# Instance norm on one core: equal 4 MB units in six slots, against 4 MB and 6 MB units in four

## The chip, the cores and the metric

The kernel runs on one core of a Trainium2 chip. The metric is the device time of one execution in microseconds (us). Three runs of the kernel before took 626.85, 626.98 and 627.24 us; the median is 626.98.

The core has five engines that work side by side and meet at semaphores: TensorE (PE, matrix products), VectorE (DVE), ScalarE (ACT), GpSimd (POOL) and SyncE (SP, which here only issues transfers). Data moves between the large memory (HBM) and the on-chip memory (128 partitions) by 16 DMA engines. SP, ACT and POOL each issue transfers into a queue of their own.

## What is computed

```python
# x: [4, 8, 16, 256, 256] float32, gamma: [8, 16] float32
mu = x.mean(axis=(3, 4), keepdims=True)
var = ((x - mu) ** 2).mean(axis=(3, 4), keepdims=True)
out = (x - mu) / np.sqrt(var + 1e-5) * gamma[None, :, :, None, None]
```

There are 512 channels (4 x 8 x 16) of 65,536 numbers, 256 KB each. Every channel gets its own mean and variance, and one of 128 values of gamma. 134 MB are read and 134 MB written, and a channel must be read whole before its first number can be written.

## The kernel before

A **unit** is 16 consecutive channels, 4 MB, held as a tile of 128 partitions by 8192 numbers: a channel is 8 partitions, and a partition holds one row of 32 KB that is contiguous in HBM. There are 32 units and six slots for them (`slots`, L45); unit `u` uses slot `u % 6`.

The program issues the first six loads at once (L56 and L57): units 1 and 3 on ACT's queue, the rest on SP's. A write of 8 KB to the output (`touch`, L54) and the load of gamma (L55) go through POOL's queue. POOL then makes `navg` (L63 to L73), a 128 by 128 matrix that holds -1/65536 where two partitions belong to the same channel, and 0 elsewhere. DVE repeats gamma (L80) and PE spreads it to a column per unit position (L85), copied to `g_col` (L91).

The loop over units is written out in one order for each engine (the schedule is manual; every engine does its own instructions in program order):

1. DVE sums each row (L106) while ACT squares each row and sums that (L107, the squares themselves go to `junk`).
2. PE multiplies `navg` by the two columns of sums (L115): every partition gets minus its channel's mean and minus its mean square.
3. DVE makes minus the variance (L116), ACT its square root (L120), DVE the reciprocal (L124) and the product with gamma (L126).
4. DVE adds minus the mean and multiplies by the scale, in place (L135). In unit 0 alone ACT does the last 3/8 of it (L132), beside DVE.
5. ACT issues the store of the unit (L139), and SP the load of unit `u + 6` (L48). That load waits until the store has landed, since it overwrites the slot.

Of the kernel before, what the change touches and what calls it, by code (L numbers as in the profile page):

```python
# [1 line left out]

# [4 lines left out]

F32 = mybir.dt.float32
U8 = mybir.dt.uint8
ALU = mybir.AluOpType  # L10
ACTF = mybir.ActivationFunctionType
AX = mybir.AxisListType


@with_exitstack
def kernel(
    ctx: ExitStack,
    tc: tile.TileContext,
    x: bass.AP,
    gamma: bass.AP,  # L20
    out: bass.AP,
):
    nc = tc.nc
    B, G, C, H, W = x.shape
    P = nc.NUM_PARTITIONS
    HW = H * W
    n_ch = B * G * C
    S = 8
    K = P // S
    F = HW // S  # L30
    U = n_ch // K
    NG = (G * C) // K
    AHEAD = 6
    assert HW % S == 0 and (G * C) % K == 0

    xv = x.rearrange("b g c h w -> (b g c h w)").rearrange("(u p f) -> u p f", p=P, f=F)
    ov = out.rearrange("b g c h w -> (b g c h w)").rearrange("(u p f) -> u p f", p=P, f=F)
    gv = gamma.rearrange("g c -> (g c)")

    data = ctx.enter_context(tc.tile_pool(name="data", bufs=1))  # L40
    singles = ctx.enter_context(tc.tile_pool(name="singles", bufs=1))
    psum = ctx.enter_context(tc.tile_pool(name="psum", bufs=4, space=bass.MemoryType.PSUM))
    ctx.enter_context(tc.manual_schedule())

    slots = [data.tile([P, F], F32, name=f"xt{i}") for i in range(AHEAD)]  # L45

    def load(u, queue):
        queue.dma_start(out=slots[u % AHEAD][:], in_=xv[u])  # L48


    g_row = singles.tile([1, G * C], F32, name="g_row")
    touch = singles.tile([16, 128], F32, name="touch")
    nc.vector.memset(touch[:], 0.0)  # L53
    nc.gpsimd.dma_start(out=ov[0][0::S, 0:128], in_=touch[:])  # L54
    nc.gpsimd.dma_start(out=g_row[:], in_=gv[None, :])  # L55
    for u in range(AHEAD):  # L56
        load(u, nc.scalar if u in (1, 3) else nc.sync)  # L57

    eps_t = singles.tile([P, 1], F32, name="eps_t")
    nc.gpsimd.memset(eps_t[:], 1e-5)  # L60
    one = singles.tile([1, 1], F32, name="one")
    nc.gpsimd.memset(one[:], 1.0)
    navg = singles.tile([P, K, S], F32, name="navg")  # L63
    nc.gpsimd.memset(navg[:], -1.0 / HW)  # L64
    nc.gpsimd.affine_select(  # L65
        out=navg[:], in_=navg[:], pattern=[[-S, K], [0, S]], compare_op=ALU.is_ge,
        fill=0.0, base=0, channel_multiplier=1,
    )
    nc.gpsimd.affine_select(  # L69
        out=navg[:], in_=navg[:], pattern=[[S, K], [0, S]], compare_op=ALU.is_ge,  # L70
        fill=0.0, base=S - 1, channel_multiplier=-1,
    )
    navg_w = navg[:].rearrange("p k s -> p (k s)")  # L73
    root_eps = singles.tile([P, 1], F32, name="root_eps")
    nc.scalar.activation(out=root_eps[:], in_=eps_t[:], func=ACTF.Sqrt)  # L75
    g_rep = singles.tile([1, NG, K, S], F32, name="g_rep")
    g_ps = psum.tile([P, NG], F32, name="g_ps", bufs=1)
    g_col = singles.tile([P, NG], F32, name="g_col")

    nc.vector.tensor_copy(  # L80
        out=g_rep[:],
        in_=g_row[:].rearrange("o (n k) -> o n k", n=NG).unsqueeze(3).to_broadcast([1, NG, K, S]),
    )
    for n in range(NG):
        nc.tensor.matmul(  # L85
            out=g_ps[:, n : n + 1],
            lhsT=g_rep[:, n].rearrange("o k s -> o (k s)"),
            rhs=one[:],
            start=True, stop=True,
        )  # L90
    nc.vector.tensor_copy(out=g_col[:], in_=g_ps[:])  # L91

    junk = singles.tile([P, F], U8, name="junk")

    st = singles.tile([P, U, 2], F32, name="st")
    nvar = singles.tile([P, U], F32, name="nvar")
    std = singles.tile([P, U], F32, name="std")
    rstd = singles.tile([P, U], F32, name="rstd")
    scale = singles.tile([P, U], F32, name="scale")

    shift = singles.tile([P, 1], F32, name="shift")

    squares = []
    for u in range(U):
        t = slots[u % AHEAD]
        nc.vector.reduce_sum(out=st[:, u, 0:1], in_=t[:], axis=AX.X)  # L106
        square = nc.scalar.activation(  # L107
            out=junk[:], in_=t[:], func=ACTF.Square, accum_out=st[:, u, 1:2],
        )
        if u:  # L110

            tc.declare_no_dep(square.ins, squares[-1].ins, reason="junk, ordered by the root between")
        squares.append(square)
        ps = psum.tile([P, 2], F32, name="ps")
        nc.tensor.matmul(out=ps[:], lhsT=navg_w, rhs=st[:, u], start=True, stop=True)  # L115
        nc.vector.tensor_scalar(  # L116
            out=nvar[:, u : u + 1], in0=ps[:, 0:1], scalar1=ps[:, 0:1],
            scalar2=ps[:, 1:2], op0=ALU.mult, op1=ALU.add,
        )
        nc.scalar.activation(  # L120
            out=std[:, u : u + 1], in_=nvar[:, u : u + 1], func=ACTF.Sqrt,
            bias=eps_t[:], scale=-1.0,
        )
        nc.vector.reciprocal(out=rstd[:, u : u + 1], in_=std[:, u : u + 1])  # L124
        g = u % NG
        nc.vector.tensor_mul(  # L126
            out=scale[:, u : u + 1], in0=rstd[:, u : u + 1], in1=g_col[:, g : g + 1],
        )
        cut = F * 5 // 8 if u == 0 else F
        if cut < F:  # L130
            nc.vector.tensor_mul(out=shift[:], in0=ps[:, 0:1], in1=scale[:, u : u + 1])  # L131
            nc.scalar.activation(  # L132
                out=t[:, cut:], in_=t[:, cut:], func=ACTF.Identity, bias=shift[:], scale=scale[:, u : u + 1],
            )
        nc.vector.tensor_scalar(  # L135
            out=t[:, :cut], in0=t[:, :cut], scalar1=ps[:, 0:1], scalar2=scale[:, u : u + 1],
            op0=ALU.add, op1=ALU.mult,
        )
        nc.scalar.dma_start(out=ov[u], in_=t[:])  # L139
        if u + AHEAD < U:  # L140
            load(u + AHEAD, nc.sync)


# [1 line left out]
_INS = ['x', 'gamma']  # L145
_OUTS = [((4, 8, 16, 256, 256), 'float32')]


# [23 lines left out]
```

## Time and profile before

| | value |
|---|---|
| median of the runs | 626.98 us |
| the profiled execution: span, first to last instruction | 625.2 us |
| DVE busy | 441.8 us (71%) |
| ACT busy | 241.8 us (39%) |
| PE busy | 21.4 us (3%) |
| POOL busy | 2.4 us |
| bytes moved by the DMA engines | 268.46 MB, mean 429 GB/s |
| packets on ACT's queue (q10) and on SP's (q1) | 4896 and 4320 |
| 4 MB store, issue to landing, median | 62.5 us |
| 4 MB load on SP, issue to landing, median | 38.5 us |

The page cuts the span into 40 equal slices of 15.6 us and gives, for each, the busy share of every engine in tenths and what the DMA engines moved. A **packet** is what one DMA engine moves at a time; here it is a row of a tile. After the rows of a transfer, each of the 16 engines sends a small completion packet of 4 bytes. A group of instructions has its busy time, the mean time of one, and the idle time of its engine before them with what ended it. The times of the profiled execution are those of its span; the runs' times also hold what lies around the span.

### The profile page before, as it was taken

The numbers are of one execution on the slowest core, as the hardware profiler recorded it, in microseconds if no ns is written. First come the engines' busy times: TensorE is split into PE (matmuls) and PEld (weight loads), VectorE is DVE, ScalarE is ACT, GpSimd is POOL, SyncE is SP. The second block draws the span as 40 slices with busy tenths as digits, with TensorE's granted clock in tenths as the row PEclk, the third lists the DMA queues.
The fourth block names the chain that finished last, engine by engine and source line by source line (L and its number), as shares of the span: only waits on it lengthen the run. The fifth ranks groups of instructions, "written<-read, shape, count | busy, mean of one in ns | idle before, by whom it ended". The sixth has DMA issues, their size and how long they took to land.

```text
span 625.2 us, 635 instructions
## 1 busy us (share of the span) xinstructions
PE 21.4 (3%) x80; PEld 19.5 (3%) x80; DVE 441.8 (71%) x164; ACT 241.8 (39%) x99; POOL 2.4 (0%) x11
## 2 busy tenths in 40 slices
PE   0200000000000000000000000000000000000000
PEld 0200000000000000000000000000000000000000
DVE  0589999998776687666786767867668676687730
ACT  0464444444443244432344423444224442244400
POOL 1000000000000000000000000000000000000000
DMA  8999999999999999999999999999999999999998
GB/s 370 436 407 432 436 436 436 436 436 430 423 436 434 434 428 434 434 436 436 436 436 428 426 436 436 432 430 434 434 436 436 436 436 421 432 436 434 434 430 367
DMA packets 9282, 268.46 MB, mean 429 GB/s; under 512 B 1072, under 2 KB 1088, under 8 KB 1088
## 3 DMA queue, kind: packets, MB, share of 16 engines
q10 hardware_dynamic: 4896, 142.61, 52.9%
q1 hardware_dynamic: 4320, 125.83, 46.8%
q0 software_dynamic: 64, 0.01, 0.0%
q14 instruction: 2, 0.02, 0.0%
HBM read 134.22 MB, written 134.23 MB: 429 GB/s over the span
## 4 chain that ended last, share of the span: by engine, by line
another core or an unknown queue 61%; DMA 17%; DVE 15%; SPq 1%; PE 1%; issue 0%; ACT 0%
DMA xt<-in_x_dram 10%; DVE st L106 10%; DMA out_dram<-xt 8%; DVE xt L135 5%; SPq L48 1%; PE ps L115 1%; ACT std L120 0%; DVE nvar L116 0%; DVE rstd L124 0%; DVE scale L126 0%; DVE shift L131 0%
## 5 line engine op out<-in xcount | busy, mean ns | idle before, releaser
L106 DVE TENSOR_REDUCE st<-xt 128x1 f32<-128x8192 f32 x32 | 277.9, 8684 | 102.2 <-DMA xt<-in_x_dram 102.2
L107 ACT ACTIVATE junk<-xt 128x8192 uint8<-128x8192 f32 x32 | 225.0, 7030 | 272.0 <-DMA xt<-in_x_dram 233.8
L135 DVE TENSOR_SCALAR xt<-xt,ps,scale 128x8192 f32<-128x8192 f32 (+1 forms) x32 | 144.0, 4500 | 1.1
L120 ACT ACTIVATE std<-nvar,eps_t 128x1 f32<-128x1 f32 x32 | 9.4, 295 | 79.4 <-DVE nvar L116 79.4
L115 PE MATMUL ps<-st,navg 128*128 128x2 f32 x64 | 17.8, 348 | 557.3 <-DVE st L106 557.3
L115 PEld LDWEIGHTS ps<-st,navg 128*128 128x128 f32 x64 | 16.0, 310 | 559.1 <-issue 546.2
L116 DVE TENSOR_SCALAR nvar<-ps 128x1 f32<-128x1 f32 x32 | 9.2, 286 | 23.8 <-PE ps L115 23.8
L124 DVE RECIPROCAL rstd<-std 128x1 f32<-128x1 f32 x32 | 5.2, 163 | 11.6 <-ACT std L120 11.6
L80 DVE COPY g_rep<-g_row 1x1024 f32<-1x1024 f32 x1 | 0.7, 681 | 14.4 <-DMA g_row<-in_gamma_dram 14.4
L107 ACT ACTIVATION_READ_ACCUMULATOR junk<-xt 128x1 f32 x32 | 6.0, 186 | 0.0
L126 DVE TENSOR_TENSOR scale<-rstd,g_col 128x1 f32<-128x1 f32 x32 | 5.1, 158 | 1.1
L85 PE MATMUL g_ps<-one,g_rep 1*128 1x1 f32 x16 | 3.5, 347 | 16.3 <-DVE g_rep L80 16.3
L85 PEld LDWEIGHTS g_ps<-one,g_rep 1*128 1x128 f32 x16 | 3.5, 326 | 16.3 <-issue 16.3
L132 ACT ACTIVATE xt<-xt,shift,scale 128x3072 f32<-128x3072 f32 x1 | 2.9, 2947 | 0.7 <-DVE shift L131 0.7
L91 DVE COPY g_col<-g_ps 128x8 f32<-128x8 f32 x1 | 0.2, 167 | 3.7 <-PE g_ps L85 3.7
L75 ACT ACT_TABLE_LOAD x1 | 1.3, 1283 | 1.7 <-PEq L156 1.7
L53 DVE MEMSET touch<- 16x128 f32 x1 | 0.2, 165 | 0.9 <-PEq L156 0.9
L54 POOL DMA_DIRECT2D out_dram<-touch x1 | 0.6, 617 | 0.8 <-DVE touch L53 0.8
L55 POOL DMA_DIRECT2D g_row<-in_gamma_dram x1 | 0.5, 487 | 0.0
L65 POOL TENSOR_SCALAR_AFFINE_SELECT navg<-navg 128x128 f32<-128x128 f32 x1 | 0.4, 400 | 0.1
L69 POOL TENSOR_SCALAR_AFFINE_SELECT navg<-navg 128x128 f32<-128x128 f32 x1 | 0.4, 399 | 0.1
L64 POOL MEMSET navg<- 128x128 f32 x1 | 0.2, 230 | 0.0
(8 smaller groups left out, 1.0 us busy)
## 6 DMA issues: line engine op xcount, KB each, us to landing
out_dram<-xt ACTq DMA_DIRECT2D x32, 4096.0 KB, 62.5
xt<-in_x_dram SPq DMA_DIRECT2D x30, 4096.0 KB, 38.5
xt<-in_x_dram ACTq DMA_DIRECT2D x2, 4096.0 KB, 31.7
out_dram<-touch POOLq DMA_DIRECT2D x1, 8.0 KB, 9.3
g_row<-in_gamma_dram POOLq DMA_DIRECT2D x1, 0.5 KB, 13.5
```

The costliest lines, as they stand in the source:

```text
L48: queue.dma_start(out=slots[u % AHEAD][:], in_=xv[u])
L75: nc.scalar.activation(out=root_eps[:], in_=eps_t[:], func=ACTF.Sqrt)
L85: nc.tensor.matmul(out=g_ps[:, n : n + 1], lhsT=g_rep[:, n].rearrange("o k s -> o (k s)"), rhs=one[:], start=True, stop=True,)
L106: nc.vector.reduce_sum(out=st[:, u, 0:1], in_=t[:], axis=AX.X)
L107: square = nc.scalar.activation(out=junk[:], in_=t[:], func=ACTF.Square, accum_out=st[:, u, 1:2],)
L115: nc.tensor.matmul(out=ps[:], lhsT=navg_w, rhs=st[:, u], start=True, stop=True)
L116: nc.vector.tensor_scalar(out=nvar[:, u : u + 1], in0=ps[:, 0:1], scalar1=ps[:, 0:1], scalar2=ps[:, 1:2], op0=ALU.mult, op1=ALU.add,)
L120: nc.scalar.activation(out=std[:, u : u + 1], in_=nvar[:, u : u + 1], func=ACTF.Sqrt, bias=eps_t[:], scale=-1.0,)
L124: nc.vector.reciprocal(out=rstd[:, u : u + 1], in_=std[:, u : u + 1])
L126: nc.vector.tensor_mul(out=scale[:, u : u + 1], in0=rstd[:, u : u + 1], in1=g_col[:, g : g + 1],)
L132: nc.scalar.activation(out=t[:, cut:], in_=t[:, cut:], func=ACTF.Identity, bias=shift[:], scale=scale[:, u : u + 1],)
L135: nc.vector.tensor_scalar(out=t[:, :cut], in0=t[:, :cut], scalar1=ps[:, 0:1], scalar2=scale[:, u : u + 1], op0=ALU.add, op1=ALU.mult,)
```

## The change

Units are no longer equal. `sizes` counts them in steps of 8 channels (2 MB): two units of 4 MB, thirteen of 6 MB, two of 4 MB, five of 6 MB, one of 4 MB; 23 units. There are four slots of 6 MB in place of six of 4 MB (24 MB in both). All loads go whole through SP's queue (`split` is empty), and the load of unit `u + 4` waits for the store of unit `u`.

A 6 MB unit has 128 rows of 48 KB: 24 channels over 128 partitions, so a channel is 5 1/3 partitions. Each row is three **pieces** of 4096 numbers, and a piece belongs to one channel. In a group of 16 partitions lie 48 pieces and three channels. DVE sums the three pieces of each row in one reduce, ACT squares them in three instructions. The mask `by_c` says which of the three channels of its group each piece belongs to; with it DVE sorts the sums to channels (`parts`, `sums`), PE sums them over the group in one product of six columns with `navg3`, and DVE picks for each piece its own channel's results (`picks`, `means`). Variance, root, reciprocal and scale are then three columns wide, and the unit is applied in three instructions of 4096 numbers. A 4 MB unit is worked as before, with `navg2`.

ACT helps DVE with the applying in unit 0 (the last 3/8, as before) and now in the last three units too (the third piece of a 6 MB unit, 3/8 of the 4 MB one). The setup is longer: POOL makes five masks in place of one (`navg2`, `navg3`, `in8`, `in16`, `owner`), one product spreads gamma to all partitions in place of eight, and 24 small DVE instructions make the masks `by_c` and `by_j` and put gamma in place for pieces (`g_piece`) and for 4 MB units (`g_col`).

The diff, cut to what the text speaks of:

```diff
-    S = 8
-    K = P // S
-    F = HW // S
-    AHEAD = 6
+    F = 4096
+    SLOTS = 4
+    sizes = [2] * 2 + [3] * 13 + [2] * 2 + [3] * 5 + [2]
+    split = {}
+    helped = (0, U - 3, U - 2, U - 1)
+    def rows(flat, u):
+        lo = starts[u] * P * F
+        return flat[lo : lo + sizes[u] * P * F].rearrange("(p f) -> p f", p=P)
...
-    slots = [data.tile([P, F], F32, name=f"xt{i}") for i in range(AHEAD)]
-    def load(u, queue):
-        queue.dma_start(out=slots[u % AHEAD][:], in_=xv[u])
+    slots = [data.tile([P, 3 * F], F32, name=f"xt{i}") for i in range(SLOTS)]
+    def home(u):
+        return slots[u % SLOTS][:, : sizes[u] * F]
+    def load(u):
+        cut = split.get(u, 0) * F
+        if cut:
+            nc.scalar.dma_start(out=home(u)[:, :cut], in_=rows(xf, u)[:, :cut])
+        if cut < sizes[u] * F:
+            nc.sync.dma_start(out=home(u)[:, cut:], in_=rows(xf, u)[:, cut:])
...
-    for u in range(AHEAD):
-        load(u, nc.scalar if u in (1, 3) else nc.sync)
+    for u in range(SLOTS):
+        load(u)
...
+    by_c = singles.tile([P, 3, 3], F32, name="by_c")
+    nc.vector.reduce_sum(
+        out=by_c[:], in_=owner[:].rearrange("p j (b k) -> p k j b", k=3), axis=AX.X,
+    )
...
     for u in range(U):
+        t = home(u)
+        three = sizes[u] == 3
+        n = sizes[u] if three else 1
+        step = sizes[u] * F // n
+        nc.vector.reduce_sum(
+            out=st[:, u, :n, 0], in_=t.rearrange("p (j f) -> p j f", j=n), axis=AX.X,
+        )
+        for j in range(n):
+            square = nc.scalar.activation(
+                out=junk[:, :step], in_=t[:, j * step : (j + 1) * step],
+                func=ACTF.Square, accum_out=st[:, u, j, 1:2],
+            )
...
+        if three:
+            nc.vector.tensor_mul(
+                out=parts[:],
+                in0=st[:, u].rearrange("p j v -> p v j").unsqueeze(1).to_broadcast([P, 3, 2, 3]),
+                in1=by_c[:].unsqueeze(2).to_broadcast([P, 3, 2, 3]),
+            )
+            nc.vector.reduce_sum(out=sums[:, u], in_=parts[:], axis=AX.X)
+            nc.tensor.matmul(
+                out=ps[:], lhsT=navg3, rhs=sums[:, u].rearrange("p k v -> p (k v)"),
+                start=True, stop=True,
+            )
+            nc.vector.tensor_mul(
+                out=picks[:],
+                in0=ps[:].rearrange("p (k v) -> p v k", v=2).unsqueeze(1).to_broadcast([P, 3, 2, 3]),
+                in1=by_j[:].unsqueeze(2).to_broadcast([P, 3, 2, 3]),
+            )
+            nc.vector.reduce_sum(out=means[:, u], in_=picks[:], axis=AX.X)
+            mean = means[:, u, :, 0]
+            nc.vector.tensor_mul(out=nvar[:, u], in0=mean, in1=mean)
+            nc.vector.tensor_add(out=nvar[:, u], in0=nvar[:, u], in1=means[:, u, :, 1])
...
+        cut = sizes[u] * F
+        if u in helped:
+            cut = 2 * F if three else cut * 5 // 8
...
+        for j in range(n):
+            lo, hi = j * step, min((j + 1) * step, cut)
+            if lo < hi:
+                nc.vector.tensor_scalar(
+                    out=t[:, lo:hi], in0=t[:, lo:hi], scalar1=mean[:, j : j + 1],
+                    scalar2=scale[:, u, j : j + 1], op0=ALU.add, op1=ALU.mult,
+                )
-        nc.scalar.dma_start(out=ov[u], in_=t[:])
-        if u + AHEAD < U:
-            load(u + AHEAD, nc.sync)
+        nc.scalar.dma_start(out=rows(of, u), in_=t)
+        if u + SLOTS < U:
+            load(u + SLOTS)
```

## The prediction

> **What bounds the kernel now.** I read the GB/s line of the page first, because 268 MB through one core is the obvious suspect, then the busy time by stretch, the waits of SyncE's queue (SP), and last the instruction groups.
>
> ```profile
> span 625.2 us, 635 instructions
> ...
> DMA  8999999999999999999999999999999999999998
> GB/s 370 436 407 432 436 436 436 436 436 430 423 436 434 434 428 434 434 436 436 436 436 428 426 436 436 432 430 434 434 436 436 436 436 421 432 436 434 434 430 367
> DMA packets 9282, 268.46 MB, mean 429 GB/s; under 512 B 1072, under 2 KB 1088, under 8 KB 1088
> ```
>
> The same by stretch (columns: length, then busy time of each engine, granted clock, DMA share, GB/s):
>
> ```profile
> 0.00:4.00 4.00, 0.00 (x0) 0.00 (x0) 0.17 (x1) 1.49 (x2) 2.39 (x11) 1.00 0.68 229
> 4.00:36.00 32.00, 4.10 (x18) 3.98 (x18) 12.90 (x8) 9.92 (x4) 0.00 (x0) 1.00 1.00 430
> 36.00:46.00 10.00, 0.56 (x2) 0.50 (x2) 9.14 (x3) 7.65 (x4) 0.00 (x0) 1.00 1.02 403
> 46.00:110.00 64.00, 2.22 (x8) 2.00 (x8) 58.99 (x23) 29.88 (x13) 0.00 (x0) 1.00 1.00 433
> 110.00:547.00 437.00, 12.81 (x46) 11.50 (x46) 319.19 (x117) 170.76 (x70) 0.00 (x0) 1.00 1.00 433
> ...
> 622.00:625.20 3.20, 0.00 (x0) 0.00 (x0) 0.00 (x0) 0.00 (x0) 0.00 (x0) 1.00 0.26 113
> ```
>
> The 16 DMA engines are full from 4 us to the end, and always move the same 433 GB/s; no compute engine is full. Against 433 GB/s the start (229 in 4 us) loses 4 x 204/433 = 1.9 us, the stretch with the first store 10 x 30/433 = 0.7 us, the end 3.2 x 320/433 = 2.4 us, and 4 to 36 us 0.2 us. These 5.2 us and 268.46 MB / 433 GB/s = 620.0 us make the span of 625.2. So 99% of the time is bytes at one rate. The change can move only (a) that rate, (b) the 5.2 us, or (c) open a hole in which no transfer is queued.
>
> **Rate.** The bytes stay, but their cut changes. Before, every row is 32 KB: 8192 packets, 512 for each DMA engine. After, ten 4 MB transfers have 128 rows of 32 KB and thirty-six 6 MB ones 128 rows of 48 KB: (10 + 36) x 128 / 16 = 368 packets per engine, 144 fewer, and 46 large transfers instead of 64. What does a packet cost beyond its bytes? Three windows of the DMA view (0.5 to 24 us long) hold three packet sizes:
>
> ```profile
> q0 software_dynamic: 16, 0.01, 2.7%
> q14 instruction: 1, 0.01, 3.9%
> q10 hardware_dynamic: 367, 10.49, 100.4%
> ```
>
> The first is 7 to 8 us: 16 packets of 512 B, 2.7% of 16 us, 27 ns each. The second is 143.7 to 144.2 us: one of 8 KB, 3.9% of 8 us, 312 ns. The third is 590 to 614.2 us, stores alone: 320 packets of 32 KB and 47 completion packets of about 9 ns in 388.7 us, 1213.5 ns each. From 512 B to 32 KB the slope is 1186.5 ns / 32256 B = 0.03678 ns per byte. The spacing, which sets the rate, is seen in the steady window:
>
> ```profile
> DMA packets 4444, 129.89 MB, mean 433 GB/s; under 512 B 480, under 2 KB 480, under 8 KB 480
> ```
>
> That is 200 to 500 us: 4444 - 480 = 3964 packets, 16 x 300 us / 3964 = 1210.9 ns per packet. 32768 B at the slope are 1205.2, so about 5.7 ns are paid per packet. **144 x 5.7 ns = 0.82 us less.** Bounds: with the slope from 8 KB to 32 KB (0.03668) the fixed part is 8.9 ns, 1.3 us less; if a 48 KB row goes as two packets, an engine has 80 + 2 x 288 = 656, 144 more, and it is 0.8 us more. No row shows 48 KB; I take 0.8, from the 512 B row, where the fixed part is largest in the total.
>
> The Trainium skill ("DMA: Bandwidth & Descriptors", "Why small descriptors are slow") gives some 3 cycles per packet on the engine's inner bus; at its 850 MHz an estimate of 3.5 ns, by which the gain would be 0.5 us. It adds that merging is worth it only at 256 B or less, which speaks against this change; the trace's 5.7 ns agrees in kind and is a little dearer.
>
> **Start, first store, end.** Loads 1 and 3 move from ACT's queue to SP's, whose first load already opens the traffic. The 1.9 us come before and with the first packets, the 0.7 us with the first store's, the 2.4 us with the last landing; all three remain, with the 8 KB touching write, and the last transfer stays 4 MB. I cost them at nothing; bounds 0 to -0.7 for the first store (its place moves), and for the start rival 4.
>
> **Holes.** The rest of the change is compute beside full DMA engines. Its cover is the queue, so I walk the slots: a 4 MB transfer is 9.7 us alone, 6 MB 14.5 us.
>
> ```profile
> L106 DVE TENSOR_REDUCE st<-xt 128x1 f32<-128x8192 f32 x32 | 277.9, 8684 | 102.2 <-DMA xt<-in_x_dram 102.2
> L107 ACT ACTIVATE junk<-xt 128x8192 uint8<-128x8192 f32 x32 | 225.0, 7030 | 272.0 <-DMA xt<-in_x_dram 233.8
> L135 DVE TENSOR_SCALAR xt<-xt,ps,scale 128x8192 f32<-128x8192 f32 (+1 forms) x32 | 144.0, 4500 | 1.1
> ```
>
> *Head.* The four first loads are 20 MB, 48.4 us of work on SP until about 50 us. DVE now has 24 small operations on gamma and the mask before its first reduce. Two wait for GpSimd's mask alone (17 setup operations after its two DMA issues, at 0.1 to 0.4 us, ready by 10 us); 22 wait for gamma, landed at 15.5 us in the trace, and one product (0.6): at 0.16 to 0.29 us, as L124 and L116 take, 6.4 us at most. So the first reduce starts by 22.5 us, as before (22.8), its store is queued by 36, 14 us before the loads run out. ACT's first store waits also for the touching write, as before. The 8 old gamma matmuls (3.5 us) become one.
>
> *Steady.* A 6 MB unit costs DVE a reduce of 8.69 x 12288/8192 = 13.0 us; eight small operations (7 x 0.17 + 0.3), the product 0.7, the root 0.3 and hand-overs 0.2, together 2.7; three applies of 4096, each 2.4 by the line through 2.94 us (5120) and 4.55 (8192), 7.1 as they overlap a little. That is **22.8 us; the DMA engines need 2 x 14.5 = 29.0 for it**. ACT's three squares (3.6 + 0.19 each) end before the reduce. So DVE waits for loads, as now. A load waits in SP's queue for its slot's store (nothing else is queued there), as now:
>
> ```profile
> SPq L48 <- DMA out_dram<-xt: 514.7, 26, 39.7
> ```
>
> With 4 slots of 6 MB instead of 6 of 4 MB, one slot is in DVE's hands and 18 MB, 43 us of work, are in flight. Neither queue needs to be full: stores alone move 433 GB/s in 590 to 614 us.
>
> *Tail.* After the last load only stores run, and they move a 6 MB unit in 14.5 us while DVE makes one in 20.6 (ACT helps). By the walk unit 21's load lands near 566, unit 22's near 590; stores 21 and 22 are queued near 587 and 604. At 604 there remain 18.6 us of data, 9.7 of them store 22, so about 8 us of store 21 still cover the hand-over. Before, the last store was queued at 600.6 with 12 us of cover. No hole; a delay of over 8 us in the last unit would show one to one.
>
> **Sum.** 625.2 - 0.8 = 624.4 us of span. The runs' median, 626.98, lies 1.8 above the profiled span; **626.2 us**.
>
> **Rivals.**
> 1. *Dearer packets, cheaper first store* (0.20): 8.9 ns per packet and no first-write loss, 1.3 + 0.7 = 2.0: 625.0. For it: the 8 KB row. Against: its window shows a single packet, and rounding alone moves it by 4 ns.
> 2. *The change doesn't do what it says* (0.08): rows of 48 KB go as two packets, 0.8 more: 627.8. All packets in the trace are whole rows, but none over 32 KB is seen.
> 3. *VectorE becomes the bound* (0.05), the slower side: the applies of a piece, whose two scalars are now single columns in SBUF, run at half rate. A piece takes 4.5 us instead of 2.4, a unit 6.5 more, 29.3 against the DMA's 29.0. It decides from 6.2 us more per unit; above that each microsecond costs 18, here 18 x 0.3 = 5 us: 632. The 5120 row at 2.94 us, with a scalar in SBUF and one in PSUM, speaks against it.
> 4. *One load queue doesn't fill the engines before the first store* (0.04): some 28 us, 23 packets per engine; it beats the gain from 36 ns per packet and shows as slower from 90 ns. The DMA view of 0 to 4 us has SP's opening 16 packets at 44.7% of 64 us, 1.79 us each, 0.58 over the later ones; at that for all 23, 13 us: 639. The lone store queue at 433 GB/s speaks against it.
> 5. *Each transfer costs a fixed time* (0.01). The page would have to show it as idle DMA between transfers; from one load's issue to the next lie 19.36 us (179.27 and 198.63), and the bytes of a load and a store at 433 GB/s take 19.37. Taken as 2 us (the end's loss) for 18 transfers: 591. [...]
>
> **Numbers.** The forecast has 0.62. The range takes in rivals 1 and 2, 625.0 to 627.9. I call a run faster or slower from 0.2% (1.25 us, under 625.7 or over 628.2), about what a measurement of this kernel can tell from no change. Faster: rivals 1 and 5 and 0.06 of the forecast, 0.27. Slower: rivals 3 and 4 and 0.01 of rival 2, 0.10. The rest, 0.63, is within.
>
> **What would show it.** Some 5,888 large packets and 433.5 to 434 GB/s in the steady slices say that the rate step is right; 10,496 that rows were cut. The DMA line without a digit below 9 between the ends says that there is no hole; a reduce, small operations and applies of 22.8 us in all against 29.0, that rival 3 is out; 430 GB/s up to the first store, that rival 4 is. What would make me wrong is a DMA rate for 48 KB rows that the packets up to 32 KB don't foretell.

## The result, and the profile after

| | before | after |
|---|---|---|
| median of 5 runs | 626.90 us (626.78 to 627.24) | 630.67 us (629.19 to 631.30) |
| ratio after / before | | 1.0055, 95% interval 1.0043 to 1.0067 |
| the profiled execution: span | 625.2 us | 628.9 us (its time is 630.67) |
| first and last of the 16 DMA engines to end their data | 622.9 and 623.9 us | 622.2 and 627.6 us |

The changed kernel is slower by 3.8 us, outside the predicted range (625.0 to 627.9). The page of the changed kernel, its span, DMA rows and instruction queue:

```profile
span 628.9 us, 717 instructions
...
DMA  8999999999999999999999999999999999999995
GB/s 367 461 411 421 425 434 447 444 410 444 447 407 447 444 410 447 444 410 447 444 410 447 447 404 433 446 419 432 448 418 449 422 444 444 425 431 446 418 431 251
DMA packets 6692, 268.48 MB, mean 427 GB/s; under 512 B 784, under 2 KB 800, under 8 KB 800
...
q14 instruction: 4, 0.03, 0.0%
```

There are 6692 - 800 = 5892 large packets (5888 rows and four of 8 KB), so the 48 KB rows go whole, as predicted. The DMA digits are 9 up to the last slice; only that one differs from before (5 for 8, and 251 GB/s for 367). The time is lost in the last 16 us, or shows there. By stretch (columns as in the prediction: length, engines, clock, DMA share, GB/s):

```profile
0.00:4.00 4.00, 0.00 (x0) 0.00 (x0) 0.17 (x1) 1.49 (x2) 2.63 (x13) 1.00 0.68 213
4.00:30.00 26.00, 1.32 (x4) 1.00 (x4) 16.88 (x30) 9.72 (x4) 2.46 (x11) 1.00 1.02 441
30.00:60.00 30.00, 1.12 (x4) 1.00 (x4) 27.86 (x12) 19.19 (x10) 0.00 (x0) 1.00 0.99 418
60.00:345.00 285.00, 5.67 (x20) 5.01 (x20) 219.47 (x127) 114.54 (x71) 0.00 (x0) 1.00 1.00 433
...
590.00:622.00 32.00, 0.56 (x2) 0.50 (x2) 12.31 (x6) 10.37 (x4) 0.00 (x0) 1.00 0.99 428
622.00:628.90 6.90, 0.00 (x0) 0.00 (x0) 0.00 (x0) 0.00 (x0) 0.00 (x0) 1.00 0.07 29
```

Against 433 GB/s the end loses 6.9 x 404/433 = 6.4 us, where the same sum gave 2.4 before. That is 4.0 us, the whole loss. The start loses 4 x 220/433 = 2.0 (1.9 before), 4 to 60 us 30 x 15/433 - 26 x 8/433 = 0.6 (0.9 before).

What moves in those last microseconds? The DMA view of the changed kernel from 622.6 to 628 us:

```profile
DMA  0505000005005000005000000005000000000000
GB/s 0 243 0 243 0 0 0 0 0 243 0 0 243 0 0 0 0 0 243 0 0 0 0 0 0 0 0 243 0 0 0 0 0 0 0 0 0 0 0 0
DMA packets 11, 0.20 MB, mean 36 GB/s; under 512 B 5, under 2 KB 5, under 8 KB 5
q10 hardware_dynamic: 11, 0.20, 8.5%
```

The same view of the kernel before, 622.6 to 625 us:

```profile
DMA packets 17, 0.03 MB, mean 14 GB/s; under 512 B 16, under 2 KB 16, under 8 KB 16
q10 hardware_dynamic: 17, 0.03, 3.5%
```

The view counts packets by their starts. Before, one row of data and the 16 completions have still to start at 622.6 us. After, six rows (the last unit's are 32 KB) and five completions have, while the other eleven engines are through and idle. The trace doesn't name a packet's engine. But in it a packet starts within a few ns of the end of the one before it on its engine, and an engine moves its eight rows and the completion packet of each transfer in order. Sorted by these two rules the packets fall into 16 chains of 368 rows (512 before), which say the same: twelve of the 16 engines end between 622.2 and 622.7 us, two at 623.1, one at 625.5 and one at 627.6. The kernel ends 1.3 us after the last of them before, 1.4 after.

The engine that ended last had 4.5 us of slow packets after 50 us: 21 of them, each 0.05 to 0.7 us too long. Fourteen are the first load row after a completion packet on that engine, and these make 3.8 of the 4.5 us. The engines that ended first had none. The completions of a store show how the lag grows: the last of the 16 engines lands behind the fifth by 0.8 us at 58 us, 1.9 at 227, 2.4 from 314 to 398 (here the 4 MB units in the middle begin), 6.0 at 472 and 5.3 at the end. Before, it is 0.3 to 1.1 us throughout. Not all of the jump to 6.0 is lost time. The completions of the loads go from 2.4 to 4.1 us at 456 and back to 2.3 at 507, since 14 engines take up their stores one packet (1.8 us) earlier from then on; of the 4.5 us of slow packets, 1.7 lie between 381 and 454 us.

Compute is not the cause (waits of SP's queue, then groups; columns as before):

```profile
SPq L66 <- DMA out_dram<-xt: 540.3, 19, 45.6
```

```profile
L178 DVE TENSOR_REDUCE st<-xt 128x3 f32<-128x12288 f32 (+1 forms) x23 | 276.6, 12025 | 111.8 <-DMA xt<-in_x_dram 111.6
...
L238 DVE TENSOR_SCALAR xt<-xt,means,scale 128x4096 f32<-128x4096 f32 x52 | 122.4, 2409 | 0.6
```

DVE waits 111.8 us for loads, so it has room; an apply of 4096 takes the 2.4 us of the prediction, and the reduce of 12288 is (276.6 - 5 x 8.68)/18 = 13.0 us. Loads wait for slots, as before.

### The profile page after: what moved, and what is told of

Read it like the earlier page. It is cut to its first block, busy times and chain, and to the rows that moved or that the text cites. A ratio compares the mean times of both kernels' runs of the same rounds, so it can differ in the third digit from the quotient of the medians.

```text
span 628.9 us, 717 instructions
## 1 busy us (share of the span) xinstructions
PE 13.7 (2%) x48; PEld 12.0 (2%) x48; DVE 451.4 (72%) x268; ACT 257.7 (41%) x147; POOL 5.1 (1%) x23
## 2 busy tenths in 40 slices
DMA packets 6692, 268.48 MB, mean 427 GB/s; under 512 B 784, under 2 KB 800, under 8 KB 800
## 4 chain that ended last, share of the span: by engine, by line
DMA 40%; another core or an unknown queue 37%; DVE 17%; ACT 1%; PE 1%; issue 1%; SPq 0%; POOL 0%; DVEq 0%; ACTq 0%
DMA out_dram<-xt 23%; DMA xt<-in_x_dram 16%; DVE st L178 10%; DVE xt L238 5%; DMA g_row<-in_gamma_dram 1%; ACT xt L231 0%; SPq L66 0%; DVE g_ch L136 0%; ACT std L220 0%; PE ps L197 0%; PE ps L212 0%; DVE rstd L223 0%; DVE scale L224 0%; DVE nvar L214 0%
## 5 line engine op out<-in xcount | busy, mean ns | idle before, releaser
L178 DVE TENSOR_REDUCE st<-xt 128x3 f32<-128x12288 f32 (+1 forms) x23 | 276.6, 12025 | 111.8 <-DMA xt<-in_x_dram 111.6
L182 ACT ACTIVATE junk<-xt 128x4096 uint8<-128x4096 f32 (+1 forms) x59 | 230.4, 3906 | 261.5 <-DMA xt<-in_x_dram 246.6
L238 DVE TENSOR_SCALAR xt<-xt,means,scale 128x4096 f32<-128x4096 f32 x52 | 122.4, 2409 | 0.6
L197 PE MATMUL ps<-sums,navg 128*128 128x6 f32 x36 | 10.2, 355 | 487.1 <-DVE sums L196 487.1
L238 DVE TENSOR_SCALAR xt<-xt,ps,scale 128x8192 f32<-128x8192 f32 (+1 forms) x5 | 19.5, 3908 | 0.1
L197 PEld LDWEIGHTS ps<-sums,navg 128*128 128x128 f32 x36 | 9.0, 310 | 488.3 <-issue 466.1
L231 ACT ACTIVATE xt<-xt,shift,scale 128x3072 f32<-128x3072 f32 (+1 forms) x4 | 13.5, 3374 | 2.7 <-DVE shift L228 2.7
L212 PE MATMUL ps<-st,navg 128*128 128x2 f32 x10 | 2.8, 348 | 90.5 <-DVE st L178 90.5
L212 PEld LDWEIGHTS ps<-st,navg 128*128 128x128 f32 x10 | 2.5, 311 | 91.0 <-issue 78.1
L214 DVE TENSOR_SCALAR nvar<-ps 128x1 f32<-128x1 f32 x5 | 1.4, 286 | 3.7 <-PE ps L212 3.7
```

Of the source, the lines that this page charges most:

```text
L178: nc.vector.reduce_sum(out=st[:, u, :n, 0], in_=t.rearrange("p (j f) -> p j f", j=n), axis=AX.X,)
L182: square = nc.scalar.activation(out=junk[:, :step], in_=t[:, j * step : (j + 1) * step], func=ACTF.Square, accum_out=st[:, u, j, 1:2],)
L197: nc.tensor.matmul(out=ps[:], lhsT=navg3, rhs=sums[:, u].rearrange("p k v -> p (k v)"), start=True, stop=True,)
L212: nc.tensor.matmul(out=ps[:, :2], lhsT=navg2, rhs=st[:, u, 0], start=True, stop=True)
L231: nc.scalar.activation(out=t[:, cut:], in_=t[:, cut:], func=ACTF.Identity, bias=shift[:, u : u + 1], scale=scale[:, u, n - 1 : n],)
L238: nc.vector.tensor_scalar(out=t[:, lo:hi], in0=t[:, lo:hi], scalar1=mean[:, j : j + 1], scalar2=scale[:, u, j : j + 1], op0=ALU.add, op1=A ...
```

## The experiments

Every ratio is against runs of the kernel before on the same chip; it is taken from means, so that a single long run moves it more than the median. "End spread" is the time from the first to the last of the 16 DMA engines' data ends in the profiled execution: 1.0 us before, 5.4 us after.

### Which part of the change

**Loads on SP alone, kernel before.** One line:

```diff
-        load(u, nc.scalar if u in (1, 3) else nc.sync)
+        load(u, nc.sync)
```

> The kernel before, with its first loads 1 and 3 on SP instead of ACT, so that loads and stores no longer start and complete at the same packet. Theory 1 (out of step: an engine that is behind loses time where a load completes in the middle of a store): 628 to 631 us, and the engines end over 3 us apart. Theory 2 (rows of 48 KB): 626.9, ends 1 us apart. Theory 3 (change of unit size in mid-run) and theory 4 (longer setup code, more instruction fetches through the DMA engines): 626.9.

Measured: 629.76 us (629.17 to 632.12, 4 runs), ratio 1.0051 [1.0031, 1.0071]; end spread 4.2 us in the profiled execution, which is the slowest of the four. Its DMA view from 624 to 630 us:

```profile
DMA  0000500500005000500050005000000000000000
...
DMA packets 22, 0.20 MB, mean 33 GB/s; under 512 B 16, under 2 KB 16, under 8 KB 16
```

Six rows of 32 KB have still to start, each alone while most engines are idle. So 48 KB rows, four slots and the new code are not needed for the loss; this edit alone costs 2.8 us (629.76 for 627.00 on the same chip). In it 14 engines run loads and stores in step (a load is complete when a store is). Two took up the first store one packet later than the rest, and just these two fall behind steadily: 0.3 us at 52 us, 1.0 at 168, 2.2 at 343, 4.3 at 575. A lag can also hold up the others. The last load had landed at 598.9 us, when the last engine had its share (4.6 us behind the first), so the last store was issued at 614.0 (600.6 in the kernel before), and in the chains the other 14 engines stand idle for 0.6 to 1.6 us ahead of it. The 4.2 us at the end are what is left after that wait.

**The new code on 4 MB units in six slots.** All of the change but the unit sizes, with loads on SP, and then with loads 1 and 3 back on ACT:

```diff
-    SLOTS = 4
+    SLOTS = 6
-    sizes = [2] * 2 + [3] * 13 + [2] * 2 + [3] * 5 + [2]
+    sizes = [2] * 32
...
-    split = {}
+    split = {1: 2, 3: 2}
```

> The changed kernel with 32 units of 4 MB in six slots: its setup, its loads on SP and its help from ACT, but rows of 32 KB and no 6 MB unit. Theory 1 (out of step): 628 to 631. Theory 2 (48 KB rows) and theory 3 (change of size): 626.9. Theory 4 (setup code): 630.

> The 4 MB version of the changed kernel (32 units, six slots, 628.2 us with all loads on SP) with loads 1 and 3 back on ACT's queue, so that the first store is queued behind a load and every DMA engine takes it up at the same packet. Theory 5 (a store that arrives at an empty queue leaves some DMA engines out of step, and those fall behind): the spread of the engines goes back to 1 us and the time to 626.7 to 627.2. Rival (the longer setup and the help at the end cost the 1.2 us): 628.2 again.

Measured: 628.24 us (628.07 to 632.35, 10 runs), 1.0026 [1.0012, 1.0040], without the last line; 627.65 us (627.45 to 627.90, 10 runs), 1.0008 [0.9999, 1.0018], with it. End spreads 2.0 and 1.7 us. By the medians the new code costs about 0.7 us and the loads' queue 0.6 here, not 2.8. In the trace of the second, the engine that ended last has two slow packets after 50 us, each right behind a fetch of instructions (66.3 and 531.8 us); so there the 0.7 us look like the second fetch on one engine, which is added alone further down.

**6 MB units without the 4 MB units in the middle:**

```diff
-    sizes = [2] * 2 + [3] * 13 + [2] * 2 + [3] * 5 + [2]
+    sizes = [2] * 2 + [3] * 20
```

> The changed kernel with units of 4 MB (2) and then 6 MB (20), no change of size in mid-run. Theory 3: the slowest engine's lag, 2.4 us at 370 us in the changed kernel, doesn't grow to 5 or 6, so 627.5 to 628. Theories 1, 2 and 4: no change, 629.5 to 631.

Measured: 628.62 us, 1.0038 [1.0015, 1.0060], but the ten runs lie from 627.45 to 634.25; end spread 1.6 us in the profiled one, which took 627.77 us and is among the faster. The median is 2.0 us better than the changed kernel's, but the two intervals overlap. The jump of the lag between 398 and 472 us is gone from the profile; in a fast run that says little. That the middle units help the lag along is not shown.

**The changed kernel with its early loads on ACT**, load 1 and then loads 1 and 3:

```diff
-    split = {}
+    split = {1: 2}
...
+    split = {1: 2, 3: 3}
```

> The changed kernel with load 1 on ACT's queue: the first store then begins about where load 3 does, and loads and stores run nearly in step from there, with the same rows of 48 KB. Theory 1: the lag stays near 1 us and the time is 626 to 627.5. Theories 2, 3 and 4: 629.5 to 631.

> The changed kernel with loads 1 and 3 on ACT's queue as before: this undoes the queue part alone. With four slots SP's queue now runs empty until store 0 has landed, so load 4 arrives at an empty queue. Theory 5: still 628 to 630.5, the engines 2 to 4 us apart. Rival (any load on ACT's queue keeps the engines together, whatever arrives later): 626 to 626.5.

Measured: 630.27 us (629.71 to 633.31, 4 runs), 1.0062 [1.0038, 1.0087], and 629.64 us (629.10 to 629.94, 5 runs), 1.0041 [1.0027, 1.0055]; end spreads 3.6 and 3.7 us. My first theory, that loads on SP alone are the cause and that moving them back cures it, falls: in the kernel before it costs 2.8 us to move them, and here it gains 1.0 at most to move them back.

### Compute, or the transfers alone

**No compute.** From unit 1 on, a unit is only loaded and stored; only unit 0 is computed. First in the one-line kernel above, then in the changed one (the second one twice):

```diff
+        if u:
+            nc.scalar.dma_start(out=rows(of, u), in_=t)
+            if u + SLOTS < U:
+                load(u + SLOTS)
+            continue
```

> The kernel before with all loads on SP, but only unit 0 is computed; all other units are stored as they were loaded, so DVE and ACT hardly touch the on-chip memory after 45 us. Theory (the drift is the DMA engines' own): single engines still fall 3 us or more behind, 628 to 631. Rival (DVE and ACT reading the landed unit slow the DMA engines): spread 1 us, 625 to 627.

> The changed kernel with only unit 0 computed, all other units stored as they were loaded: the same transfers in the same order without compute. Theory: single engines fall 3 us or more behind, 628.5 to 631. Rival: spread 1 us, 626.

> The transfers of the changed kernel without compute after unit 0 and without a fetch, timed this time. If fetches and compute together make the drift: 626.8 to 627.3 in all runs. If the drift is chance (which engine starts late): as far apart as the changed kernel's runs, 627 to 630.

Measured: 626.55 us (one run), 626.94 us (one run), and of the same kernel again 629.91 us (626.87 to 632.33, 6 runs), 1.0046 [1.0022, 1.0069]. End spreads 0.6, 1.8 and 6.9 us. The last stretch of the third one's profiled execution (632.11 us):

```profile
590.00:622.00 32.00, 0.00 (x0) 0.00 (x0) 0.00 (x0) 0.00 (x0) 0.00 (x0) 1.00 0.99 427
622.00:630.40 8.40, 0.00 (x0) 0.00 (x0) 0.00 (x0) 0.00 (x0) 0.00 (x0) 1.00 0.06 23
```

No engine but the DMA engines works, no instruction is fetched after unit 0 (its page has no q14 row), and the tail is there all the same, longer than in the changed kernel. So the changed kernel's transfers make such a lag by themselves, and it varies from run to run. The single run of 626.94 had misled me: from it I would have blamed the compute. For the one-line kernel the compute is not acquitted to the same degree: with it all four runs took 629.17 us or more, without it (timed again below) seven of twelve took 626.5 to 627.2.

**Passes of 8 columns.** All instructions stay, but from unit 1 on the big passes touch 8 columns:

```diff
+        w = 8 if u else step
...
-            out=st[:, u, :n, 0], in_=t.rearrange("p (j f) -> p j f", j=n), axis=AX.X,
+            out=st[:, u, :n, 0], in_=t.rearrange("p (j f) -> p j f", j=n)[:, :, :w], axis=AX.X,
```

> The changed kernel with every instruction kept, but from unit 1 on the large passes (sums, squares, applying) touch only 8 columns of each piece: all transfers and all four fetches, and hardly any reading of the on-chip memory by VectorE and ScalarE. If the drift is the DMA engines' own, started by fetches: 629.5 to 631, slowest engine 4 us or more behind. If the compute's own traffic drives it: 627 to 628, 2 us or less beyond the two fetches' 0.8 each.

Measured: 629.78 us (627.18 to 630.60, 7 runs), 1.0037 [1.0025, 1.0050], end spread 4.7 us. So the changed kernel loses its time without the traffic of DVE and ACT on the tiles, too.

### Instruction fetches

After has four fetches of 8 KB of instructions, before two. Each goes to one DMA engine, takes it 0.31 us and is followed there by a data packet up to 0.54 us longer. They come back to the same engine: in the changed kernel at 85.7 and 371.5 us on one, at 176.3 and 593.1 us on another.

**More small instructions**, four per unit in the kernel before and six in the changed one:

```diff
+        for i in range(4):
+            nc.vector.memset(pad[:, i : i + 1], 0.0)
```

> The kernel before with four more one-column VectorE instructions a unit, in VectorE's idle time (128 in all), which bring one more instruction fetch through a DMA engine. Theory 6 (each fetch puts one DMA engine 0.8 us behind, and with loads and stores in step it stays that far behind and no farther): the page shows 3 instruction packets instead of 2, the slowest engine is 1.7 us behind instead of 0.9, and the time is 0.7 to 0.9 us longer, 627.6 to 627.9. Rival (a fetch costs nothing in the end): 626.9 to 627.0.

> The changed kernel with six more one-column VectorE instructions a unit (138 in all), which bring one more fetch. Theory 7 (out of step, an engine that is behind falls farther behind): more than the 0.8 us of the fetch itself, 631.5 to 634. Rival (only the fetches' own time counts, in step or not): 0.7 to 0.9 us longer than the changed kernel, 631.2 to 631.6. Rival 2 (the drift has nothing to do with fetches): 630.5.

Measured, first: 627.67 us (627.56 to 628.34, 11 runs), 1.0011 [1.0002, 1.0020]; three fetches, two of them on one engine (81 and 348 us), whose lag steps from 1.2 to 2.1 us and then stays. The DMA view from 622.6 to 626 us:

```profile
DMA  0080000000000800000000000000000000000000
...
DMA packets 18, 0.07 MB, mean 19 GB/s; under 512 B 16, under 2 KB 16, under 8 KB 16
```

One row more is left than in the kernel before, on an engine by itself. A second fetch on the same engine costs the end 0.7 us. Second kernel: 629.92 us (629.50 to 630.05, 4 runs), 1.0045 [1.0030, 1.0060], with five fetches and an end spread of 4.6. By the time, a fifth fetch made no more drift. In the profiled execution of the changed kernel the engine that ended last had no fetch, and one execution of the transfers alone (632.11 us) lags by 6.9 us without any. So the lag doesn't need a fetch. But fetches often choose the engine: of the ten profiled executions with the new code's instructions, the changed kernel's is the only one in which the engine that ended last had not taken two or three of them (three in this run, 2.4 us with the packets behind them, of a spread of 4.6). In the changed kernel and in that execution it was an engine already 0.6 to 0.7 us behind the middle one at 40 us. That an engine which is behind by such an amount falls farther behind would fit both, but no run sets out to show it, and none takes the fetches out of a complete kernel.

### The moment at which the stores join the loads

What is left is how the two streams lie against each other on the DMA engines. I counted how many packets of a store an engine has sent when a load is complete on it: 8 of 8 on every engine in the kernel before, 2 of 8 in the changed kernel. The moment of store 0 sets this number at the start, and it stays until a later store shifts it (to 3 of 8 on 14 engines, behind the 4 MB units in the middle).

**The changed kernel's transfers alone, store 0 at two other moments.** DVE's and PE's work on gamma and masks and all other compute is left out (POOL's setup and the load of gamma stay); unit 0 has one or two reduces as a delay and a pass of 8 columns, so its store is issued at 20.03 or at 23.49 us (30.68 in the changed kernel):

```diff
-            nc.vector.reduce_sum(out=wait[:, 0:1], in_=t[:, :5900], axis=AX.X)
+            nc.vector.reduce_sum(out=wait[:, 0:1], in_=t[:, :8192], axis=AX.X)
+            nc.vector.reduce_sum(out=wait[:, 1:2], in_=t[:, :1040], axis=AX.X)
```

> Transfers of the changed kernel alone (no compute; unit 0 only waits), store 0 issued at about 19.8 us instead of 30.6, so that every DMA engine should take its first packet right after the first packet of load 2: a load and a store then always end at the same packet. Step theory: all runs within 625.4 to 626.4 us, no engine falls farther behind. Rows theory (48 KB rows make engines drift): 627 to 632 and scattered, as before.

> The same, store 0 issued two packets (3.6 us) later, at about 23.4 us, nothing else changed. Step theory: 626.5 to 632, scattered over more than 1.5 us. Rows theory: the same as e13.

Measured: 714.69 us (712.89 to 716.42, 4 runs), 1.1395 [1.1379, 1.1412], and 626.84 us (625.63 to 627.16, 11 runs), 0.9994 [0.9985, 1.0002]. The page of the first kernel:

```profile
span 714.7 us, 159 instructions
...
DMA  9999999999999999999999999999999999998985
GB/s 382 420 426 421 380 385 391 371 391 366 388 377 382 377 377 396 369 358 399 349 388 360 374 366 349 361 338 368 376 425 434 370 377 385 374 371 340 364 373 226
```

The page of the second:

```profile
span 625.4 us, 160 instructions
...
DMA  8999999999999999999999999999999999999997
GB/s 369 417 436 432 425 453 446 409 450 428 431 450 406 453 446 409 450 428 431 450 406 453 446 409 435 451 419 436 433 423 449 439 431 424 453 402 453 419 453 322
```

The transfers, their sizes, order, queues and slots are the same. Both are full of 9s, so idle engines don't explain it: the packets themselves are slow. The durations of the data packets from 100 to 345 us:

| | loads: median, mean ns | over 2% too long (beyond 1213 or 1815) | stores: median, mean ns | over 2% too long |
|---|---|---|---|---|
| before (32 KB) | 1213, 1213.5 | 0.1% | 1213, 1213.8 | 1.0% |
| after | 1815, 1817.0 | 1.1% | 1815, 1815.5 | 0.1% |
| store 0 at 20.03 us | 1815, 2072.5 | 39.9% | 1919, 2065.9 | 53.7% |
| store 0 at 23.49 us | 1815, 1815.1 | 0.1% | 1815, 1815.1 | 0.0% |

With the store at 20.03 us a load is complete on most engines when 8 of 8 packets of a store have gone: the streams are in step. With 23.49 it is 6 of 8. I had expected the state in step to be the harmless one, since there no engine drifted in the one-line kernel without compute; with 48 KB rows it is by far the worst, on all engines at once. And with 48 KB rows and another moment, nothing is lost. So neither 48 KB rows nor the loads' queue are the cause by themselves; in these transfers it is the moment of store 0, and with it how the loads and stores lie against each other, that decides.

**The same on 32 KB rows,** the one-line kernel without compute, store 0 as it comes and three packets later (32.31 us):

```diff
+        nc.vector.reduce_sum(out=wait[:], in_=t[:, :3300], axis=AX.X)
```

> The same without the delay, timed: where all engines are in step, 626.4 to 626.7 by both theories; runs in which an engine or two take the first store a packet late would be 1 to 4 us longer by the step theory.

> The kernel before with all loads on SP and only unit 0 computed (626.55 us in one run, in step), store 0 delayed by three packets of 32 KB (3.6 us). Step theory: 627 to 632, scattered. Rows theory: 626.3 to 626.8.

Measured: 627.15 us (626.53 to 630.49, 12 runs), 1.0016 [1.0002, 1.0030], in step; 626.91 us (626.60 to 627.18, 11 runs), 0.9997 [0.9988, 1.0005], three packets later. With 32 KB rows, in step costs nothing in most runs; five of the 12 lie at 628.6 to 630.5, where the run out of step has none.

**The complete changed kernel, store 0 later.** One more reduce on DVE ahead of unit 0's apply, of 3580 or of 6890 columns:

```diff
+        if u == 0:
+            nc.vector.reduce_sum(out=wait[:], in_=t[:, :3580], axis=AX.X)
```

> The whole changed kernel, with one more reduce of 3580 columns (3.8 us of VectorE) in unit 0 ahead of its apply, so that store 0 is issued near 34.5 us instead of 30.7. Theory 10 (the time goes by the moment at which the stores join the loads; one packet of 48 KB is 1.81 us, and the pattern repeats after 8 packets, 14.5 us): 34.5 is 14.5 after the 20.03 of the run with loads and stores in step (714.7), so a load should be complete when 8 or 0 packets of the store have gone, and the kernel should be much slower, 640 to 720 us. Rival A (the changed kernel loses its 3.8 us to its compute, its fetches or the 4 MB units, wherever the stores start): 629 to 632. Rival B (only the delay counts, one to one, as the first store's place): 634.

> The same with 6890 columns (7.3 us), store 0 near 38.0 us: 14.5 us after the 23.49 of the run that took 626.84. Theory 10: a load is complete when 6 packets of the store have gone, no engine drifts, and the whole changed kernel takes 626.5 to 628 us, the second fetch of instructions on one engine included. Rival A: 629 to 632. Rival B: 638.

Measured: 630.17 us (628.84 to 630.75, 4 runs), 1.0047 [1.0034, 1.0060], and 629.48 us (627.16 to 633.09, 9 runs), 1.0045 [1.0025, 1.0064]. Both expectations of the theory failed as times; the traces tell why. In the first, store 0 is issued at 34.20 us, and the streams do fall in step (8 of 8 at 62 us). By stretch:

```profile
37.00:46.00 9.00, 0.56 (x2) 0.50 (x2) 7.83 (x5) 5.04 (x3) 0.00 (x0) 1.00 0.88 348
46.00:92.00 46.00, 1.16 (x4) 1.00 (x4) 43.21 (x24) 22.85 (x14) 0.00 (x0) 1.00 1.00 417
92.00:345.00 253.00, 5.09 (x18) 4.51 (x18) 187.78 (x108) 102.81 (x63) 0.00 (x0) 1.00 1.00 434
```

The changed kernel itself has 402 and 434 GB/s in the first two of these stretches. So in step the complete kernel is slow too, 417 GB/s. But a store that waits for compute comes late at 94 us, the streams come apart (4 of 8 from there on), and at 434 GB/s nothing more is lost. The price is 46 x 17/433 = 1.8 us on all engines; the first of them ends at 623.7 us for 622.2, and the end spread is 3.2 us. In the second kernel the reduce had to wait for ACT's share of the same tile, so store 0 came at 40.88 us and not at the 38 that I aimed at. A load is then complete at 4, later 3 of 8 packets, and one engine lags by 3.4 us at the end. The moment that was harmless for the transfers alone has not been reached in the complete kernel, so that it would cure the complete kernel is not shown.

## Why the prediction was wrong, step by step

- **Rate: right.** Predicted 0.82 us less. The five engines that ended first did so at 622.19 to 622.24 us after and 622.91 to 623.06 before, 0.72 us less between the first ones; by 144 packets, 5.0 ns each where I took 5.7. The Trainium skill ("DMA: Bandwidth & Descriptors", "Why small descriptors are slow") gives 3 cycles, by my estimate 3.5 ns; this measurement lies between the two. Rival 1 (8.9 ns) and rival 2 (rows cut in two) are out. I had named the rate of 48 KB rows as what would make me wrong; in this kernel it came as foretold.
- **Start, first store, end: this is the step that failed.** "All three remain ... I cost them at nothing". The first two did remain: 2.0 for 1.9, and 0.6 for 0.9. (My bound of 0 to -0.7 held for the first store's own loss; that its moment, 30.68 us for 36.48, could cost something later was not in it.) The end went from 2.4 to 6.4 us. I had read its 2.4 us as the landing of the last transfer. It also holds the spread of 16 engines, 1.0 us then, since a transfer has landed when the slowest of them has. The spread went to 5.4: 4.4 more, less the 0.7 of the rate, is the 3.7 us by which the span grew. I gave this term no upper bound at all, because I worked with one rate for 16 engines. The Trainium skill says what I should have drawn from ("DMA: Bandwidth & Descriptors", "Why a DMA increments its semaphore by 16 and not by 1"): the count climbs by one as each engine's data lands. The trace agrees: the sixteen completions of one transfer lie up to 6.3 us apart.
- **Holes: right.** The DMA digits stay at 9; DVE has its slack, with reduces of 13.0 and applies of 2.4 us. What I called the cover of the tail was not drawn on.
- **Rival 3 (VectorE) and rival 4 (one load queue) are out:** the applies run at full rate, and from 4 to 30 us one load queue moves 441 GB/s. Rival 4 looked at the right edit for the wrong reason. Moving loads 1 and 3 to SP does cost, 2.8 us in the kernel before, but not at the start: there the lag comes over the next 600 us, on two engines whose loads and stores lie one packet apart from the others'.
- **Median against span: right,** 630.67 - 628.9 = 1.8 us.

What is shown: the loss is the lag of single DMA engines; the changed kernel's transfers make such a lag alone, without compute after unit 0 and without fetches; a lag comes with 32 KB rows too (629.76 us) and can be absent with 48 KB rows (626.84); for the same transfers, the moment of the first store moves the time from 626.84 to 629.91 and 714.69 us. A repeated fetch on one engine adds 0.7 us in the kernel before, where small instructions in idle time were added to bring it.

What stays open: why a packet becomes slow when the streams lie so, why on two engines here, on all of them there, and how much of a complete kernel's lag starts with a fetch. Reads and writes that meet at the memory would fit. The Trainium skill ("DMA: Bandwidth & Descriptors", "Latency and other measured facts") reports copies falling from 214 to 103 GB/s at row pitches of large powers of two, and gives channels hit in lock step as an unverified reason; the rows here lie 32 and 48 KB apart and no run varied that alone, so that is a candidate and no more. Nor is it shown how much of the changed kernel's lag is the 4 MB units in the middle (1.7 us of slow packets around them in one profile, but the kernel without them scatters up to 634), nor that a complete kernel with 6 MB units can reach 626. No complete version here beat the kernel before; the nearest, new code on 4 MB units with loads 1 and 3 on ACT, took 627.65 us.

## What to carry to other kernels

When the DMA engines are full from end to end, read them as 16 engines and not as one rate: look at what is left after the first of them has ended, and give that term its own bound in any forecast. A change that only shifts when the first store joins the loads can cost more than the packets it saves, so vary that moment by a few packets before judging a transfer size (in the complete kernel here the two later moments that were tried gave 630.17 and 629.48 us, no cure). And take several runs of any kernel whose result is to acquit or to blame something: one run of 626.94 us stood for a kernel whose others went to 632.33.

## What the runs showed of the hardware

- Loads and stores of 48 KB rows in step took 2.07 us a packet on average for 1.815, and the same transfers ran 14% longer (714.69 us for 626.84) when the first store came 3.5 us earlier.
- With all queues full, one DMA engine of 16 can fall behind by 4 to 7 us in 600, by packets 0.05 to 0.9 us too long (4.2 us in the one-line kernel, 5.4 in the changed one, 6.9 in its transfers alone). No other engine takes over its rows: in the chains each moves eight rows of every transfer.
- A fetch of 8 KB of instructions holds one DMA engine for 0.31 us, the packet after it is up to 0.54 us longer, and a later fetch can come to the same engine: 0.7 us at the end for the second (626.96 to 627.67).
